# A decoder layer on one core: the norm's gain moved back into the weights, five leading chunks, and the sums of squares multiplied out later

## The chip, the core and the metric

The kernel runs on one NeuronCore of a Trainium2 chip. The core has a matrix engine (TensorE, called PE in the profile, with its weight loads as PEld), a vector engine (DVE), a scalar engine (ACT), a general engine (POOL) and a queue engine (SP) that issues DMAs. Each runs its own queue of instructions in order and waits for the others on semaphores. Results of PE go to eight PSUM banks; everything else lies in SBUF. The metric is the device time of one execution in microseconds; lower is better.

## The reference

One layer of a hybrid decoder, for a prompt of 1024 tokens and 8 sequences of 4 sample tokens (1056 token columns together), model width 1024, all in float32:

```python
h = x * rsqrt(mean(x*x) + EPS) * norm_g
b_g, c_g, u, z_a, v, z_b = split(h @ w_in)        # 1024 -> 6 x 512
y_a = b_g * conv3(c_g * u) * silu(z_a)            # three taps along the tokens
pooled = window_mean(v) - v                       # windows 2, 4, 8, 16 for four groups of 128
y_b = (pooled @ pool_w[group]) * pool_scale * silu(z_b)
out = rmsnorm(x + concat(y_a, y_b) @ w_out) * final_g
```

The last rows of `c_g*u` and of `v` are returned as new states. The row factor `rsqrt(...)` belongs to a token, `norm_g` to an input channel. So `norm_g` can be multiplied into x or into the rows of `w_in`, and the row factor can be applied after the projection.

## The kernel before, in words

**Numbers in two halves.** Every float32 operand of a product is split into a high half, which ACT writes with a copy in the rounded format fp32r, and a low half, which DVE writes as operand minus high half (`split2`, L155 to L158). A product takes three passes: high by low, low by high, high by high.

**The input projection.** Its 24 tiles of 128 output channels are taken in 12 pairs (`PAIRS`, L35). Tokens are cut in three ranges of 352 columns, n0, n1 and n2. Pair zero (v and z_b of group 0) is done straight, chunk by chunk of 128 input channels as they arrive: `project_first` (L190), chunks in four DMA groups of 1, 2, 2 and 3 (`GROUPS`, L109). Each chunk of x is multiplied with its gain while it is split (`split_x`, L169 to L173). Ranges n2 and n0 go along with the DMAs; n1 follows.

**Pairs one to eleven** use Strassen's scheme (Winograd's form) on n0 and n1 and plain products on n2. The weights of a pair (`wraw`, 1 MB, one buffer) give four split units: a and b from the weights, c and d from their differences `tw` (`make_t`, L207 to L216: one instruction of 1024 columns, two of 512). The x side needs A11, A12, A22 and the combinations S1 to S4, made once. On PE a block is 12 products of 352 columns. Pair p runs, in `strassen` (L418):

- block B11 with A11 into bank a; ACT copies it to s1 (L440)
- block T2 with S2 into bank b; DVE writes t1 = b + s1 (L444)
- block T1 with S1 into bank c
- a plain product of 24 into bank l (L450 multiplies it with the row factors)
- block B21 with A12 into a; L452 multiplies it with the row factors
- block T3 with S3 into b, which overwrites what t1 was read from; DVE writes t2 = b + s1 (L455)
- the second plain product into bank r; then T4 with A22 into b, B22 with S4 into c

In between, the hooks `early`, `middle` and `late` (L615 on) load the weights of pair p+1 and prepare its units.

**The row factors.** Rows of x are squared and summed on ACT for five tiles of 128 tokens (`square_rows`, L248). For the rest, ACT squares x in its other layout (`squares_head`, `squares_last`), DVE adds up (`sums_last`, `sums_head`), and PE sums over the partitions (`sums_rest`, L280 to L287). `rows` (L289) makes from this the factors and nine diagonal tiles; `rows_out` (L311) spreads them over the partitions with a product and copies them to R, and R squared to R2. This happens in pair two: sums right behind T1, row products behind the first plain product. Then `scale_heads` (L593) scales what pairs zero and one had left unscaled, and `after_u(0)` and `after_v(0)` do the convolution and the pooling of it.

**What sets the order.** Up to the end of pair one, PE, ACT, DVE and POOL follow the order of the text (`manual_schedule`, L489). From pair two on only PE does (L641); the instructions of ACT and DVE are put in order by the scheduler of the framework when the program is built, which mostly lets earlier text go first and fills holes with what is ready. The blocks of a pair are written behind one another; between the two parts the scheduler had already mixed some products of pair two's first block among the last of pair one.

Of the kernel before, what the change touches and what calls it, by code (L numbers as in the profile page):

```python
# [7 lines left out]
F32 = mybir.dt.float32  # L8
F32R = mybir.dt.float32r
AF = mybir.ActivationFunctionType  # L10
# [3 lines left out]
P = 128  # L14
# [18 lines left out]


PAIRS = [(("v", 0), ("zb", 0)), (("c", 0), ("u", 0)), (("za", 0), ("b", 0)),  # L35
# [3 lines left out]
NP = len(PAIRS)  # L39
M_ORDER = [t for pair in PAIRS for t in pair]  # L40
NF = 2
M_BASE = {"b": 0, "c": 512, "u": 1024, "za": 1536, "v": 2048, "zb": 2560}

E_ORDER = [0, 4, 7, 1, 6, 2, 5, 3]

WF = NF * P + 1

# [15 lines left out]
def trunk(ctx, tc, xt, xres, xct, w_first, w_in, w_out, pool_w, par, fg, sconv, spool,  # L63
# [17 lines left out]
    def tmp(name, dtype=F32):  # L81
        return tp.tile([P, TOK], dtype, tag="tmp", name=name)

    def snap(name):
        return sp.tile([P, TN], F32, tag="snap", name=name)

    def bank(name):
        return ps.tile([P, 512], F32, tag="ps", name=name)
# [17 lines left out]
        nc.sync.dma_start(raw[n][:, k:k + m, :], xt[:, n * KD + k:n * KD + k + m, :])  # L106


    GROUPS = ((0, 1), (1, 2), (3, 2), (5, 3))  # L109
    for k, m in GROUPS:  # L110
        nc.sync.dma_start(wfraw[:, k:k + m, :], w_first[:, k:k + m, :])
        for n in (2, 0):
            load_x(n, k, m)
# [41 lines left out]
    def split2(hi, lo, src):  # L155

        nc.scalar.activation(hi, src, AF.Copy)  # L157
        nc.vector.tensor_tensor(lo, src, hi.bitcast(F32), op=ALU.subtract)  # L158
# [7 lines left out]
    pl = [xtile("xh", "pl_0"), xtile("xi", "pl_1")]  # L166
    blocks = {(0, 0): A11, (0, 1): A12, (1, 0): A21, (1, 1): A22, (2, 0): pl[0], (2, 1): pl[1]}

    def split_x(n, k, g):  # L169
        dst, src = blocks[n, k // KH], raw[n][:, k]  # L170
        hi, lo = (dst[:, a, k % KH] for a in range(2))
        nc.scalar.activation(hi, src, AF.Copy, scale=g)
        nc.vector.scalar_tensor_tensor(lo, src, g, hi.bitcast(F32), op0=MUL, op1=SUB)  # L173


    def wtile(i, shape, name, dtype=F32R):
# [1 line left out]

    w0 = [wtile(h, [P, 2, KH, 2 * P], f"w0_{h}") for h in range(2)]

    def prep_w0(k0, m):
        for h in range(2):
            a, b = max(k0, h * KH), min(k0 + m, (h + 1) * KH)
            if a < b:
                q = slice(a - h * KH, b - h * KH)
                split2(w0[h][:, 0, q], w0[h][:, 1, q], wfraw[:, a:b, :2 * P])

    pm = {}

# [11 lines left out]


    unit = {}
    slot = {}
    tw = {}

    def make_t(p, steps=(0, 1)):  # L207
        w = wraw[p]
        if 0 in steps:
            tw[p] = wp.tile([P, 4, KH * P], F32, tag="tw", name=f"tw_{p}")  # L210
        t = tw[p]
        if 0 in steps:
            vt(t[:, 0:2], w[:, 2:4], w[:, 0::2], op=SUB)
        if 1 in steps:
            vt(t[:, 2], w[:, 3], t[:, 0], op=SUB)
            vt(t[:, 3], w[:, 1], t[:, 2], op=SUB)  # L216

    def make_unit(p, u):
        if p not in slot:
# [195 lines left out]

    def strassen(p, S1, S2, S3, S4, hooks):  # L418
        (q, j), (_, _) = PAIRS[p]
        if q == "v":  # L420
# [7 lines left out]
            left, right = tmp(f"z_{j}"), tmp(f"y_{j}")  # L428
            scale = R

        def plain(i, name):
            pt = bank(name)[:, :TN]
            block(pt, p, ("B11", "B12")[i], pl[0], True, False)
            block(pt, p, ("B21", "B22")[i], pl[1], False, True)
            return pt

        a = bank(f"a_{p}")[:, :TN]
        s1 = snap(f"s1_{p}")
        block(a, p, "B11", A11, True, False)
        nc.scalar.copy(s1, a)  # L440
        b = bank(f"b_{p}")[:, :TN]
        block(b, p, "T2", S2, True, False)
        t1 = snap(f"t1_{p}")
        vt(t1, b, s1, op=ADD)  # L444
        c = bank(f"c_{p}")[:, :TN]
        block(c, p, "T1", S1, True, False)
        hooks.get("rest", lambda: None)()
        pL = plain(0, f"l_{p}")
        hooks.get("rows", lambda: None)()
        vt(left[:, n2], pL, scale[:, n2], op=MUL)  # L450
        block(a, p, "B21", A12, False, True)
        vt(left[:, n0], a, scale[:, n0], op=MUL)  # L452
        block(b, p, "T3", S3, False, False)
        t2 = snap(f"t2_{p}")
        vt(t2, b, s1, op=ADD)  # L455
        vt(right[:, n1], c, t2, op=ADD)
        hooks["early"]()
        pR = plain(1, f"r_{p}")
        if q == "v":
            vt(right[:, n2], pR, R[:, n2], op=MUL)  # L460
        elif q == "c":
# [25 lines left out]
    szb[0] = tmp("szb_0")  # L487
    heads = [vb[:, PM:], szb[0]]
    with tc.manual_schedule(engines={ET.PE, ET.Activation, ET.DVE, ET.Pool}):  # L489
        for k0, m in GROUPS:  # L490
            prep_w0(k0, m)
            for k in range(k0, k0 + m):
                for n in (2, 0):
                    split_x(n, k, wfraw[:, k, 2 * P:])
                    project_first(n, k)
        nc.vector.tensor_copy(gain.rearrange("p (k o) -> p k o", o=1), wfraw[:, :, 2 * P:])
        gk = [gain[:, k:k + 1] for k in range(KD)]
        load_w(1)
        nc.sync.dma_start(part, par)
        xk = [load_rows(t, q[:, :D]) for t, q in enumerate((R, R2, up[:, 2:]))]  # L500
        slot[1] = {"a": 2, "b": 3, "d": 4, "c": 0}
        slot[2] = {"a": 1, "d": 2, "c": 0, "b": 4, "spare": 3}
        acc = tmp("acc")
        for k in range(KD):
            split_x(1, k, gk[k])
            project_first(1, k)
        sh = squares_head(acc)

        S3f, S2f, S1f = raw[1][:, :KH], raw[1][:, KH:], raw[0][:, :KH]
        vt(S3f, raw[0][:, :KH], raw[1][:, :KH], op=SUB)  # L510
        make_unit(1, "a")
        for k in range(KH):
            nc.scalar.activation(S3f[:, k], S3f[:, k], AF.Copy, scale=gk[k])
        for k in range(KH):
            nc.vector.scalar_tensor_tensor(S2f[:, k], S2f[:, k], gk[KH + k], S3f[:, k], op0=MUL, op1=SUB)
        make_t(1)
        make_unit(1, "b")
        for i in range(2):
            nc.scalar.copy(heads[i][:, n2], pm[i, 2])
        sq = squares_last()  # L520
        make_unit(1, "d")
        S2 = xtile("xa", "S2")
        split(S2, S2f)
        S3 = xtile("xb", "S3")
        split(S3, S3f)
        make_unit(1, "c")
        x34 = wtile(1, [P, 2, D], "x34", F32)
        xk += [load_rows(t, x34[:, t - 3]) for t in (3, 4)]
        load_w(2)
        for k in range(KH):  # L530
            nc.vector.scalar_tensor_tensor(S1f[:, k], S1f[:, k], gk[k], S2f[:, k], op0=MUL, op1=ADD)
        for t in (3, 4, 2):
            square_rows(t, xk[t])


        t_0, um = tmp("t_0"), up[:, 2:]

        def plain1(i):
            pt = bank(f"lr{i}_1")[:, :TN]
            block(pt, 1, ("B11", "B12")[i], pl[0], True, False)  # L540
            block(pt, 1, ("B21", "B22")[i], pl[1], False, True)
            return pt

        pL = plain1(0)
        pa, pb, pc = (bank(f"{q}_1")[:, :TN] for q in "abc")
        s1, t1, t2 = (snap(f"{q}_1") for q in ("s1", "t1", "t2"))
        block(pa, 1, "B11", A11, True, False)
        nc.scalar.copy(s1, pa)
        pR = plain1(1)
        block(pa, 1, "B21", A12, False, True)  # L550
        S4f = [tp.tile([P, 2, TN], F32, tag="tmp", name=f"S4f_{h}") for h in range(2)]
        for k in range(KH):
            nc.vector.scalar_tensor_tensor(S4f[k // 2][:, k % 2], raw[0][:, KH + k], gk[KH + k], S2f[:, k],
                                           op0=MUL, op1=SUB)
        S1 = xtile("xc", "S1")
        split(S1, S1f)
        make_unit(2, "a")
        for n in (0, 1):
            for i in range(2):
                nc.scalar.copy(heads[i][:, cols[n]], pm[i, n])  # L560
        block(pb, 1, "T2", S2, True, False)
        vt(t1, pb, s1, op=ADD)
        S4 = xtile("xd", "S4")
        for h in range(2):
            ks = slice(2 * h, 2 * h + 2)
            split2(S4[:, 0, ks], S4[:, 1, ks], S4f[h])
        block(pc, 1, "T1", S1, True, False)
        nc.scalar.copy(t_0[:, n2], pL)
        make_t(2, (0,))
        nc.scalar.copy(t_0[:, n0], pa)  # L570
        block(pb, 1, "T3", S3, False, False)
        vt(t2, pb, s1, op=ADD)
        vt(um[:, n1], pc, t2, op=ADD)
        make_t(2, (1,))
        make_unit(2, "d")
        for t in range(2):
            square_rows(t, xk[t])
        block(pb, 1, "T4", A22, False, True)
        vt(t_0[:, n1], pb, s1, op=ADD)
        make_unit(2, "c")  # L580
        block(pc, 1, "B22", S4, False, True)
        vt(um[:, n0], pc, t1, op=ADD)
        for _ in sums_last(acc, sq):
            pass
        sums_head(acc, sh)
        make_unit(2, "b")
        vt(up[:, 2 + 2 * TN:], pR, t_0[:, n2], op=MUL)
        vt(up[:, 2:2 + 2 * TN], um[:, both], t_0[:, both], op=MUL)
# [23 lines left out]
    def pair(p):  # L612
        nxt = p + 1 < NP

        def early():  # L615
            if nxt:
                load_w(p + 1)
                make_t(p + 1)
                make_unit(p + 1, "a")

# [235 lines left out]
```

## Time and profile before

| | us |
|---|---|
| runs | 380.45, 380.75, 379.07 (median 380.45) |
| the profiled execution | 380.98 |
| its span, first to last instruction | 379.2 |
| PE busy, share of the span | 367.1, 97% |
| DVE busy | 278.8, 74% |
| ACT busy | 147.0, 39% |
| mean granted clock of PE | 0.982 |

How to read it: all rows come from one execution. A row of instructions gives its start and length in us, the engine, the line, the operation, what it writes and reads, and in brackets how long the engine had been idle before it and what ended that. A row of a group (`... x11 | 13.4, 1221 |`) gives the count, the sum in us and the mean in ns. A row of a stretch (`60.00:62.00 ...`) gives its length, then the busy time of PE, PEld, DVE, ACT and POOL with their counts, the granted clock, the share of the DMA engines and GB/s. The chain rows give start, length and what the end of the execution hung on. A DMA row ends with the KB and the us from issue to landing. Instructions that follow on one engine overlap by some 0.09 us, so that four of 574 ns take 2.0 us.

### The profile page before, as it was taken

Reading aid. Unit: us, or ns where it says so; the run is one execution under the profiler, and the core shown is the slowest. Engines: PE = TensorE matmul, PEld = TensorE weight load, DVE = VectorE, ACT = ScalarE, POOL = GpSimd, SP = SyncE. Lnnn points to the kernel's source line nnn. Section 1 sums busy time; section 2 is a strip of 40 time slices with the busy share of each in tenths; the row PEclk is TensorE's granted clock in tenths of the full one; section 3 lists DMA queues with packets and bytes.
Section 4 is the critical chain, followed back from the end, with each engine's and each line's share of the span. In section 5 each row is a group of like instructions: output and inputs, shape, how many; then the busy total and the mean of one; then the engine's idle time right before and its main releaser. Section 6 shows DMA issues by size and latency. Waiting matters only on the chain.

```text
span 379.2 us, 5200 instructions
## 1 busy us (share of the span) xinstructions
PE 367.1 (97%) x2114; PEld 353.4 (93%) x2114; DVE 278.8 (74%) x433; ACT 147.0 (39%) x231; POOL 1.4 (0%) x7
## 2 busy tenths in 40 slices
PE   6999997999999999999999999999999999999993
PEld 3999996999999999999999999999998889999883
DVE  3899869799999986769797666969269628222593
ACT  4899751863323323133332322332069215111212
POOL 0000000000000000000000000000000000000000
PEclk9899997899999999999999999999999999999998
DMA  7975002111131310303040130404639923100042
GB/s 226 394 258 190 34 0 67 73 33 80 57 112 58 112 57 19 150 2 111 0 169 0 54 137 11 165 3 129 270 110 349 417 89 124 45 0 2 0 180 111
DMA packets 13079, 41.67 MB, mean 110 GB/s; under 512 B 3712, under 2 KB 4224, under 8 KB 11648
## 3 DMA queue, kind: packets, MB, share of 16 engines
q1 hardware_dynamic: 12912, 41.02, 29.2%
q8 instruction: 16, 0.26, 0.3%
q10 hardware_dynamic: 144, 0.33, 0.2%
q14 instruction: 7, 0.06, 0.0%
HBM read 32.92 MB, written 8.42 MB: 109 GB/s over the span
## 4 chain that ended last, share of the span: by engine, by line
PE 93%; DVE 3%; DMA 2%; ACT 1%; SPq 0%; issue 0%; DVEq 0%
PE b L238 16%; PE po L686 15%; PE l L238 11%; PE a L238 11%; PE c L238 10%; PE r L238 10%; PE pc L756 10%; PE pm L196 6%; PE lr L238 2%; PE pp L392 2%; DMA raw<-in_xt_dram 2%; ACT R L249 1%; PE rest L285 0%; DVE wc L158 0%; DVE sq L274 0%; ACT wd L157 0%
## 5 line engine op out<-in xcount | busy, mean ns | idle before, releaser
L686 PE MATMUL po<-wo,mix 128*128 128x512 f32 (+1 forms) x264 | 56.5, 374 | 0.0
L686 PEld LDWEIGHTS po<-wo,mix 128*128 128x128 f32 x264 | 46.3, 188 | 9.7 <-DVE mix L158 0.2
L238 PE MATMUL a<-A,wa 128*128 128x352 f32 x264 | 46.4, 324 | 0.0
L238 PEld LDWEIGHTS a<-A,wa 128*128 128x128 f32 x264 | 43.3, 188 | 0.0
L238 PE MATMUL l<-pl,wa 128*128 128x352 f32 x240 | 42.5, 335 | 0.0
L238 PEld LDWEIGHTS l<-pl,wa 128*128 128x128 f32 x240 | 41.0, 197 | 0.0
L238 PE MATMUL r<-pl,wb 128*128 128x352 f32 x240 | 40.4, 324 | 0.0
L238 PEld LDWEIGHTS r<-pl,wb 128*128 128x128 f32 x240 | 39.1, 188 | 0.0
L756 PE MATMUL pc<-mix,wo 128*128 128x416 f32 x192 | 36.5, 351 | 0.0
L756 PEld LDWEIGHTS pc<-mix,wo 128*128 128x128 f32 x192 | 35.9, 188 | 0.5
L238 PE MATMUL c<-S,wc 128*128 128x352 f32 x132 | 23.4, 324 | 0.0
L238 PE MATMUL c<-S,wb 128*128 128x352 f32 x132 | 23.1, 324 | 0.0
L238 PE MATMUL b<-S,wc 128*128 128x352 f32 x132 | 23.1, 324 | 0.0
L238 PE MATMUL b<-S,wd 128*128 128x352 f32 x132 | 23.1, 324 | 0.0
L238 PE MATMUL b<-A,wd 128*128 128x352 f32 x132 | 23.1, 324 | 0.0
L157 ACT ACTIVATE wd<-tw 128x1024 fp32r<-128x1024 f32 x11 | 11.7, 1062 | 28.4 <-PE a L238 20.7
L238 PEld LDWEIGHTS c<-S,wc 128*128 128x128 f32 x132 | 21.6, 188 | 0.3 <-DVE wc L158 0.3
L238 PEld LDWEIGHTS b<-S,wc 128*128 128x128 f32 x132 | 21.7, 188 | 0.0
L238 PEld LDWEIGHTS c<-S,wb 128*128 128x128 f32 x132 | 21.7, 188 | 0.0
L238 PEld LDWEIGHTS b<-S,wd 128*128 128x128 f32 x132 | 21.7, 188 | 0.0
L238 PEld LDWEIGHTS b<-A,wd 128*128 128x128 f32 x132 | 21.7, 188 | 0.0
L758 DVE TENSOR_TENSOR zc<-pc,zc 128x416 f32<-128x416 f32 x8 | 4.7, 591 | 18.6 <-PE pc L756 18.6
(198 smaller groups left out, 530.7 us busy)
## 6 DMA issues: line engine op xcount, KB each, us to landing
wraw<-in_w_in_dram SPq DMA_DIRECT2D x11, 1024.0 KB, 4.7
woraw<-in_w_out_dram SPq DMA_DIRECT2D x8, 512.0 KB, 5.6
zt<-in_xres_dram SPq DMA_DIRECT2D x5, 512.0 KB, 6.2
spill_b<-yb SPq DMA_DIRECT2D x4, 528.0 KB, 2.8
mixraw<-spill_b SPq DMA_DIRECT2D x4, 528.0 KB, 6.4
out_yt_dram<-zt SPq DMA_DIRECT2D x4, 512.0 KB, 2.6
zc<-in_xct_dram SPq DMA_DIRECT2D x4, 416.0 KB, 7.2
out_yc_dram<-zc SPq DMA_DIRECT2D x4, 416.0 KB, 2.4
```

Of the source, the lines that this page charges most:

```text
L157: nc.scalar.activation(hi, src, AF.Copy)
L196: nc.tensor.matmul(pm[i, n], w0[k // KH][:, a, k % KH, i * P:(i + 1) * P], blocks[n, k // KH][:, b, k % KH], start=k == 0 and s == 0, stop ...
L238: nc.tensor.matmul(pt, t[:, a, i, k * P:(k + 1) * P], x[:, b, k], start=first and s == 0, stop=last and s == len(seq) - 1, skip_group_chec ...
L249: nc.scalar.activation(xk, xk, AF.Square, accum_out=ss[:, t:t + 1])
L392: nc.tensor.matmul(pt[:, :TN], pws[:, a, g, :], pooled[g][b][:, cols[n]], start=(s == 0), stop=(s == 2))
L686: nc.tensor.matmul(pt, mix[k][:, b, t * P:(t + 1) * P], wo[k][:, a, c], start=(k == 0 and s == 0), stop=(k == KD - 1 and s == 2))
L756: nc.tensor.matmul(pt, wo[k][:, a, d * P:(d + 1) * P], mix[k][:, b, T0:], start=(k == 0 and s == 0), stop=(k == KD - 1 and s == 2))
L758: nc.vector.tensor_tensor(zc[d], pt, zc[d], op=ALU.add)
```

## The change

- **Gain.** x is split as it is. The first weights are multiplied with the gain while they are split (`prep_w0(k)`, chunk by chunk); for pairs one to eleven a new `gain_w(p)` multiplies the loaded weights in place, eight ACT instructions of 2 x 128 columns, ahead of `make_t` and of unit a. The scaled combinations of x become plain sums and differences, in larger pieces.
- **Chunks.** The leading DMA groups are 1, 1, 1, 2, 3.
- **Pair one.** S1 and the four parts of S4 are made earlier; the x rows of tiles 3 and 4 are loaded behind the squaring of tiles 0 and 1 into the same buffers; the second weights are loaded earlier; copies and squarings stand in another order. s1, t1 and t2 of pair one use the result tiles, so that pair two's first block (`first_a`) can be written ahead of pair one's T4.
- **Pair two.** The sums' products stand behind the first plain product instead of ahead of it; the row products stand in the middle of the second plain product; the two multiplications with R that stood ahead of it come behind it.
- **Groups of v.** Pairs three, six and nine take groups 1, 3, 2 instead of 3, 2, 1. Group g has g + 1 window sums.

```diff
-         (("v", 3), ("zb", 3)), (("c", 1), ("u", 1)), (("za", 1), ("b", 1)),
-         (("v", 2), ("zb", 2)), (("c", 2), ("u", 2)), (("za", 2), ("b", 2)),
-         (("v", 1), ("zb", 1)), (("c", 3), ("u", 3)), (("za", 3), ("b", 3))]
+         (("v", 1), ("zb", 1)), (("c", 1), ("u", 1)), (("za", 1), ("b", 1)),
+         (("v", 3), ("zb", 3)), (("c", 2), ("u", 2)), (("za", 2), ("b", 2)),
+         (("v", 2), ("zb", 2)), (("c", 3), ("u", 3)), (("za", 3), ("b", 3))]
...
-    GROUPS = ((0, 1), (1, 2), (3, 2), (5, 3))
-    for k, m in GROUPS:
+    for k, m in ((0, 1), (1, 1), (2, 1), (3, 2), (5, 3)):
...
+    def gain_w(p):
+        for k in range(KD):
+            t = wraw[p][:, 0::2] if k < KH else wraw[p][:, 1::2]
+            t = t[:, :, k % KH * P:(k % KH + 1) * P]
+            nc.scalar.activation(t, t, AF.Copy, scale=gain[:, k:k + 1])
...
-        hooks.get("rest", lambda: None)()
-        pL = plain(0, f"l_{p}")
-        hooks.get("rows", lambda: None)()
-        vt(left[:, n2], pL, scale[:, n2], op=MUL)
+        pL = plain(0, f"l_{p}")
+        hooks.get("rest", lambda: None)()
+        late = "rows" in hooks
+        if not late:
+            vt(left[:, n2], pL, scale[:, n2], op=MUL)
         block(a, p, "B21", A12, False, True)
-        vt(left[:, n0], a, scale[:, n0], op=MUL)
+        if not late:
+            vt(left[:, n0], a, scale[:, n0], op=MUL)
...
-        pR = plain(1, f"r_{p}")
+        pR = plain(1, f"r_{p}", hooks.get("rows"))
+        if late:
+            vt(left[:, n2], pL, scale[:, n2], op=MUL)
+            vt(left[:, n0], a, scale[:, n0], op=MUL)
...
-        for k0, m in GROUPS:
-            prep_w0(k0, m)
-            for k in range(k0, k0 + m):
-                for n in (2, 0):
-                    split_x(n, k, wfraw[:, k, 2 * P:])
-                    project_first(n, k)
+        for k in range(KD):
+            prep_w0(k)
+            for n in (2, 0):
+                split_x(n, k, 1)
+                project_first(n, k)
...
+        vt(S2f, raw[1][:, KH:], S3f, op=SUB)
+        vt(S1f, raw[0][:, :KH], S2f, op=ADD)
+        gain_w(1)
+        make_t(1)
         make_unit(1, "a")
...
+        S1 = xtile("xc", "S1")
+        split(S1, S1f)
+        gain_w(2)
         pR = plain1(1)
...
+        first_a(2)
         block(pb, 1, "T4", A22, False, True)
...
                 load_w(p + 1)
+                gain_w(p + 1)
                 make_t(p + 1)
                 make_unit(p + 1, "a")
```

More of the change, by code (lines that the diff above doesn't have):

```diff
@@ L42 @@
 M_BASE = {"b": 0, "c": 512, "u": 1024, "za": 1536, "v": 2048, "zb": 2560}
-E_ORDER = [0, 4, 7, 1, 6, 2, 5, 3]
+E_ORDER = [0, 4, 5, 1, 7, 2, 6, 3]
 WF = NF * P + 1
@@ L167, in trunk, with split_x @@
     blocks = {(0, 0): A11, (0, 1): A12, (1, 0): A21, (1, 1): A22, (2, 0): pl[0], (2, 1): pl[1]}
[L169 to L173, printed above, removed]
+    def split_x(n, k, m):
+        dst = blocks[n, k // KH]
+        ks = slice(k % KH, k % KH + m)
+        split2(dst[:, 0, ks], dst[:, 1, ks], raw[n][:, k:k + m])
     def wtile(i, shape, name, dtype=F32R):
@@ L179, in trunk, with prep_w0 @@
     w0 = [wtile(h, [P, 2, KH, 2 * P], f"w0_{h}") for h in range(2)]
[L181 to L186, printed above, removed]
+    def prep_w0(k):
+        t, q = w0[k // KH], k % KH
+        src, g = wfraw[:, k, :2 * P], wfraw[:, k, 2 * P:]
+        nc.scalar.activation(t[:, 0, q], src, AF.Copy, scale=g)
+        nc.vector.scalar_tensor_tensor(t[:, 1, q], src, g, t[:, 0, q].bitcast(F32),
+                                       op0=ALU.mult, op1=ALU.subtract)
     pm = {}
@@ L203, in trunk @@
     unit = {}
-    slot = {}
     tw = {}
+    def gain_w(p):
[3 more added lines that the diff above has]
+            nc.scalar.activation(t, t, AF.Copy, scale=gain[:, k:k + 1])
     def make_t(p, steps=(0, 1)):
@@ L216, in make_t @@
             vt(t[:, 3], w[:, 1], t[:, 2], op=SUB)
+    slot = {}
     def make_unit(p, u):
@@ L414, in after_u, with first_a @@
         keep["yc"] = yc
+    begun = {}
+    def first_a(p):
+        a = bank(f"a_{p}")[:, :TN]
+        s1 = snap(f"s1_{p}")
+        block(a, p, "B11", A11, True, False)
+        nc.scalar.copy(s1, a)
+        begun[p] = a, s1
     def strassen(p, S1, S2, S3, S4, hooks):
@@ L429, in strassen, with plain @@
             scale = R
-        def plain(i, name):
+        def plain(i, name, hook=None):
             pt = bank(name)[:, :TN]
             block(pt, p, ("B11", "B12")[i], pl[0], True, False)
+            if hook:
+                hook()
             block(pt, p, ("B21", "B22")[i], pl[1], False, True)
             return pt
[L437 to L440, printed above, removed]
+        if p not in begun:
+            first_a(p)
+        a, s1 = begun[p]
         b = bank(f"b_{p}")[:, :TN]
@@ L489, in trunk @@
     with tc.manual_schedule(engines={ET.PE, ET.Activation, ET.DVE, ET.Pool}):
-        for k0, m in GROUPS:
-            prep_w0(k0, m)
-            for k in range(k0, k0 + m):
-                for n in (2, 0):
-                    split_x(n, k, wfraw[:, k, 2 * P:])
-                    project_first(n, k)
+        for k in range(KD):
[3 more added lines that the diff above has]
+                project_first(n, k)
         nc.vector.tensor_copy(gain.rearrange("p (k o) -> p k o", o=1), wfraw[:, :, 2 * P:])
-        gk = [gain[:, k:k + 1] for k in range(KD)]
         load_w(1)
@@ L503, in trunk @@
         acc = tmp("acc")
+        for k in range(0, KD, 2):
+            split_x(1, k, 2)
         for k in range(KD):
-            split_x(1, k, gk[k])
             project_first(1, k)
@@ L510, in trunk @@
         vt(S3f, raw[0][:, :KH], raw[1][:, :KH], op=SUB)
+        vt(S2f, raw[1][:, KH:], S3f, op=SUB)
+        vt(S1f, raw[0][:, :KH], S2f, op=ADD)
+        gain_w(1)
+        make_t(1)
         make_unit(1, "a")
[L512 to L516, printed above, removed]
         make_unit(1, "b")
-        for i in range(2):
-            nc.scalar.copy(heads[i][:, n2], pm[i, 2])
+        load_w(2)
+        for n in (2, 0):
+            for i in range(2):
+                nc.scalar.copy(heads[i][:, cols[n]], pm[i, n])
         sq = squares_last()
         make_unit(1, "d")
+        S4f = [tp.tile([P, 2, TN], F32, tag="tmp", name=f"S4f_{h}") for h in range(2)]
+        for h in range(2):
+            ks = slice(2 * h, 2 * h + 2)
+            vt(S4f[h], raw[0][:, KH:][:, ks], S2f[:, ks], op=SUB)
         S2 = xtile("xa", "S2")
@@ L526, in trunk @@
         make_unit(1, "c")
[L527 to L533, printed above, removed]
         t_0, um = tmp("t_0"), up[:, 2:]
@@ L545, in trunk @@
         pa, pb, pc = (bank(f"{q}_1")[:, :TN] for q in "abc")
-        s1, t1, t2 = (snap(f"{q}_1") for q in ("s1", "t1", "t2"))
+        s1, t1, t2 = t_0[:, n1], um[:, n0], um[:, n1]
         block(pa, 1, "B11", A11, True, False)
         nc.scalar.copy(s1, pa)
+        square_rows(2, xk[2])
+        S1 = xtile("xc", "S1")
+        split(S1, S1f)
+        gain_w(2)
         pR = plain1(1)
         block(pa, 1, "B21", A12, False, True)
[L551 to L560, printed above, removed]
+        make_t(2, (0,))
         block(pb, 1, "T2", S2, True, False)
         vt(t1, pb, s1, op=ADD)
+        make_t(2, (1,))
         S4 = xtile("xd", "S4")
@@ L566, in trunk @@
             split2(S4[:, 0, ks], S4[:, 1, ks], S4f[h])
+        make_unit(2, "a")
+        for i in range(2):
+            nc.scalar.copy(heads[i][:, n1], pm[i, 1])
         block(pc, 1, "T1", S1, True, False)
         nc.scalar.copy(t_0[:, n2], pL)
-        make_t(2, (0,))
         nc.scalar.copy(t_0[:, n0], pa)
+        for t in range(2):
+            square_rows(t, xk[t])
+        xk += [load_rows(t, xk[t - 3]) for t in (3, 4)]
         block(pb, 1, "T3", S3, False, False)
         vt(t2, pb, s1, op=ADD)
+        make_unit(2, "d")
         vt(um[:, n1], pc, t2, op=ADD)
[L574 to L577, printed above, removed]
+        first_a(2)
         block(pb, 1, "T4", A22, False, True)
@@ L582, in trunk @@
         vt(um[:, n0], pc, t1, op=ADD)
+        for t in (3, 4):
+            square_rows(t, xk[t])
         for _ in sums_last(acc, sq):
```

## The prediction

> **What bounds the kernel now.** I read the page's head first, then the busy time by stretches, then the chain of waits in order of time.
>
> ```profile
> span 379.2 us, 5200 instructions
> PE 367.1 (97%) x2114; PEld 353.4 (93%) x2114; DVE 278.8 (74%) x433; ACT 147.0 (39%) x231; POOL 1.4 (0%) x7
> ```
> ```profile
> 6.50:9.00 2.50, 0.00 (x1) 0.00 (x0) 0.70 (x2) 1.22 (x2) 0.00 (x0) 1.00 0.98 354
> 11.00:12.00 1.00, 1.00 (x6) 1.00 (x5) 1.00 (x3) 1.00 (x4) 0.00 (x0) 0.50 1.05 427
> 60.00:62.00 2.00, 0.00 (x0) 0.00 (x0) 1.90 (x5) 0.00 (x0) 0.00 (x0) 0.87 0.00 0
> 62.30:68.30 6.00, 5.99 (x23) 5.96 (x24) 5.20 (x19) 2.57 (x11) 0.00 (x0) 0.50 0.59 217
> 82.60:280.40 197.80, 197.80 (x1226) 197.80 (x1225) 155.64 (x222) 61.66 (x80) 0.00 (x0) 1.00 0.23 83
> ```
> ```profile
> 32.09 3.88 PE lr L238 x24
> 35.97 1.94 PE a L238 x12
> ...
> 62.03 0.23 DVE acc L262
> ...
> 62.31 1.64 PE rest L285 x8
> 63.95 6.05 PE l L238 x24
> 70.00 0.97 PE pr L315 x6
> ...
> 82.61 1.94 PE a L238 x12
> ```
>
> PE is 97% busy. A block of 12 products takes 1.94 us and a plain product of 24 takes 3.88 us. From 82.6 us on PE never waits until the tail, so the change moves the end only by what it moves up to there, or by waits that it newly makes behind it. Ahead of 82.6 us PE loses time in two places. At 6.5 us it waits 2.5 us for the second chunk, and the clock is at 0.50 a little later. At about 59.5 us it waits 2.8 us for the sums of squares, and the granted clock is then 0.50 for 6 us: the first plain product of pair two takes 6.05 us in place of 3.88.
>
> **The change part by part.** *Leading chunks and gain in the first weights.* The rows:
>
> ```profile
> raw<-in_xt_dram SPq DMA_DIRECT2D x1, 176.0 KB, 2.5
> raw<-in_xt_dram SPq DMA_DIRECT2D x1, 352.0 KB, 5.8
> ```
> ```profile
> 15.44 0.59 ACT L172 ACTIVATE A<-raw,wfraw 128x352 fp32r<-128x352 f32 x1 [0.71 <-DMA raw<-in_xt_dram]
> 18.55 0.16 DVE L496 COPY gain<-wfraw 128x8 f32<-128x8 f32 x1
> 24.07 1.06 ACT L157 ACTIVATE wa<-wraw 128x1024 fp32r<-128x1024 f32 x1 [0.85 <-DMA wraw<-in_w_in_dram]
> ```
> ```profile
> L513 ACT ACTIVATE raw<-raw,gain 128x352 f32<-128x352 f32 x4 | 2.0, 574 | 0.0
> L157 ACT ACTIVATE w<-wfraw 128x256 fp32r<-128x256 f32 x3 | 1.1, 407 | 1.0 <-DMA wfraw<-in_w_first_dram 1.0
> L268 ACT ACTIVATE sq<-raw 128x1056 f32<-128x1056 f32 x2 | 2.1, 1084 | 0.0
> L519 ACT COPY szb<-pm 128x352 f32<-128x352 f32 x1 | 0.4, 447 | 0.0
> L213 DVE TENSOR_TENSOR tw<-wraw 128x1024 f32<-128x1024 f32 x11 | 13.4, 1221 | 2.5 <-DMA wraw<-in_w_in_dram 2.5
> L215 DVE TENSOR_TENSOR tw<-wraw,tw 128x512 f32<-128x512 f32 x11 | 7.6, 687 | 0.1
> L158 DVE TENSOR_TENSOR wa<-wraw,wa 128x1024 fp32r<-128x1024 f32 x11 | 13.4, 1221 | 0.2 <-ACT wa L157 0.2
> L158 DVE TENSOR_TENSOR S<-raw,S 128x1408 fp32r<-128x1408 f32 x3 | 4.8, 1623 | 1.6 <-ACT S L157 1.5
> ```
>
> Chunk one alone lands between 2.5 us after its issue (the single chunk) and 5.8 us (the double one); three more DMAs pass SP. I take the middle, about 7.0 us: PE starts again near 7.7 instead of 9.0, seven chunks of 1.94 us follow, and the last 48 products (7.8 us) end at 29.0. Bounds: 28.5 to 31.9, the latter no gain at all. But the next gate does not come sooner. The last x chunk still lands at 15.4, since the bytes are the same; behind it ACT now also prepares the weights of chunks six and seven, and its last half is done at 15.4 + 0.5 + 2 x 1.3 = 18.6, the gain copy on DVE at 19.35 (18.71 before). The first weights of pair one wait for that copy, because they use the same buffer, and take 5.3 us from issue (issued right behind the copy, they let ACT start at 24.07), so they land at 24.7.
>
> Now eight ACT products with the gain come first. No row shows one of 256 columns; the scaled one of 352 takes 574 ns, four in 2.0 us, the unscaled one of 256 takes 407 ns. Eight cost 2.7 us by the one and 3.9 us by the other; I take 3.1, nearer to the one of the same width. Then 24.7 + 3.1 = 27.8; the differences of the weights (1.22 + 2 x 0.69) end at 30.5 and the low half of the first unit (1.22) at 31.7. Pair one thus starts at 31.7 against 32.09: the start's gain is taken by a new wait of up to 2.7 us at this place.
>
> *Pair one.* In this order DVE goes on from 31.7: a low half (1.1), a wait for ACT to 34.9 (four copies of 0.4 and three squarings of 1 us now stand ahead of the next high half there), a low half, 1.6 for S4, two of 1.6 for S2 and S3, a low half, and at 42.1 the low half of S1, which needs ACT's high half behind S3: 43.8. ACT's second eight gain products lie at 42.0 to 45.2, then on DVE 1.2 + 0.5 + 1.4 (weight differences and t1), 1.7 (S4), 1.2 (unit a of pair two): 50.9. PE has by then waited 1.8 us for the moved first block of pair two. From 50.9 it runs five blocks (9.7) and the plain product that now lies ahead of the sums: 64.5. The sums on DVE, which took from 57.7 to 62.25 before (rows below and above, t1 of pair two among them), start near 57.4 now and end near 61.0. So that wait of 2.8 us and its slow clock go; the sums' products then take about 1.0 us at full clock, half of 1.64 and a little. They end at 65.5; before it was 63.95. Unknown: 1.5 us either way from the start's landing times, which go through the DVE queue unshortened.
>
> *The row scales.* What they still need, and what follows, stands in these rows:
>
> ```profile
> 57.74 1.25 DVE L274 TENSOR_TENSOR sq<-sq,sq 128x1056 f32<-128x1056 f32 x1
> ...
> 66.36 2.66 ACT L307 ACTIVATE diag<-ident,rh 128x128 fp32r<-128x128 f32 x9
> 69.59 1.23 DVE L213 TENSOR_TENSOR tw<-wraw 128x1024 f32<-128x1024 f32 x1 [1.20 <-DMA wraw<-in_w_in_dram]
> 70.36 1.17 ACT L316 COPY R<-pr 128x352 f32<-128x352 f32 x3 [1.34 <-PE pr L315]
> 84.38 2.10 PE L238 MATMUL b<-S,wd 128*128 128x352 f32 x12
> 92.37 0.52 DVE L444 TENSOR_TENSOR t<-b,s 128x352 f32<-128x352 f32 x1
> 94.09 2.10 PE L238 MATMUL b<-S,wc 128*128 128x352 f32 x12
> ```
> ```profile
> 69.60:92.40 22.80, 22.80 (x143) 22.80 (x142) 22.20 (x31) 13.69 (x21) 0.00 (x0) 1.00 0.13 47
> 82.60:94.10 11.50, 11.50 (x74) 11.50 (x73) 11.50 (x19) 5.96 (x9) 0.00 (x0) 1.00 0.26 93
> ```
>
> From the sums' products to the last diagonal it is 66.36 + 2.66 - 63.95 = 5.1 us, so 70.6 now; PE meanwhile has three blocks (5.8 us) and comes at 71.4: no wait. Three more blocks and the 0.97 of the row products put the end of pair two at 78.2, against 82.61: 4.4 us ahead.
>
> *Where it is given back.* DVE is the engine to look at behind this point. Between 69.6 and 92.4 it is busy 22.2 of 22.8 us, and what it does last there is the sum t1 of pair three (L444), which PE's block T3 of that pair overwrites and so waits for. It ends at 92.9; T3 starts at 94.1. PE can gain **1.2 us and no more** unless DVE starts this list sooner or orders it otherwise. It starts later. The list opens with the weight differences of pair three, and these now wait for eight gain products on ACT, which stand behind nine diagonals: 70.7 + 3.1 = 73.9 instead of 69.6. The copies of R come after the row products at 72.3, on the same ACT queue: 73.8 to 76, instead of 70.4 to 71.5, and most of the list needs R. Two sums of pair two (2 x 0.45) are done ahead of it. So t1 starts at 73.9 + 22.2 - 0.9 = 95.2, or 94.7 where holes close, and T3 starts at 95.3 to 95.8 where it was 94.1: **1.4 us later than before**. PE is there six blocks later than 78.2 (94.25 - 82.61 = 11.6), at 89.8, and waits more than 5 us.
>
> What the clock makes of that wait: idle stretches of 2.5 and 2.8 us were each followed by a clock near 0.5, once for about 3.4 us (a loss of 1.7) and once for 6.8. Here 0 to 2.8 us can be lost; I take 1.4. The Trainium skill (TensorE: Matmul & The Clock Gate, Part 1) has the clock halved after at least one idle window of about 3.4 us, in free-running windows. This trace is harsher: 2.8 us idle was enough. By that rule a wait of 5 us costs one window at half rate, 1.7 us where the sum has 1.4.
>
> *Gain products in the later pairs.* Eight per pair, 3.1 us of ACT. The cover:
>
> ```profile
> 154.80 1.06 ACT L157 ACTIVATE wa<-wraw 128x1024 fp32r<-128x1024 f32 x1 [2.84 <-DMA wraw<-in_w_in_dram]
> 157.76 0.69 DVE L216 TENSOR_TENSOR tw<-wraw,tw 128x512 f32<-128x512 f32 x1
> 161.26 1.06 ACT L157 ACTIVATE wd<-tw 128x1024 fp32r<-128x1024 f32 x1 [1.11 <-PE a L238]
> 172.64 2.10 PE L238 MATMUL b<-S,wd 128*128 128x352 f32 x12
> ```
>
> Weights that land at 154.8 would have their differences at 160.6 instead of 158.4; the unit made of them waits for PE until 161.26 in any case, and PE wants it at 172.6. Nothing is paid; without this cover it would be 3.1 us in each of nine pairs.
>
> *Order of the groups.* The group with four windows leaves the crowded pair three, the one with two takes its place: two window sums less of 1.23 us and their small ones, some 3 us of DVE, but behind t1 of pair three. It helps pair four, where PE had no wait: nothing.
>
> **Sum.** Against the profiled execution (380.98 us, 0.53 above the median of 380.45; span 379.2): +1.4 for T3 of pair three, +1.4 for the clock, nothing behind it: 383.8, or 383.2 on the scale of the median. Own range 381 to 386.
>
> **Rivals.** *Faster: the backlog does not bind.* Behind pair one only PE's order is written by hand; DVE's is chosen by the scheduler. If it places t1 and t2 of pair three ahead of the heads' scaling, done before PE comes at 89.8, the 4.4 us stay: 376.1, or 378 with half of them kept. For it: PE's part in this list is earlier. Against: t1 had been ready since T2 ended at 86.5, and ran at 92.37: older work went first.
>
> *No change: the list starts on time.* If the head runs 1.5 us faster than my sum and PE's wait stays under 2 us, the full slack of 1.2 is kept or lost again to a short slow clock: 379.3 to 381.5, say 380.3.
>
> *Slower still: gain products ahead of the diagonals.* The third weights land as far behind pair two's last unit as before (some 6 us), near 68.2, when the diagonals start (65.5 + 2.4). If they go first on ACT, the row products wait 3 us, R comes at 76, and T3 at 96.8: 380.45 + 2.7 + 2 = 385.
>
> **How the numbers follow.** Forecast 0.50, faster 0.25, no change 0.17, slower still 0.08. A measurement of this kernel tells 0.5%, 1.9 us, from no change. Slower: 0.40 of the forecast's 0.50 and the 0.08: 0.48. Faster: 0.25 and 0.02 of the no-change case: 0.27. The same: the rest, 0.25. The range for 8 in 10 leaves out the fullest gain and ends at the forecast's upper end: 377.5 to 386.
>
> **What would show it.** The first plain product of pair one starts near 31.7 behind `wa`, not near 29. No wait of PE at the sums (L285 of before). Pair two ends near 78. Then a wait of PE of 4 to 6 us on a DVE `t` in pair three, and a granted clock of 0.5 behind it. If PE runs through pair three without a wait, my backlog is wrong and the kernel is faster; if it waits in every pair on `tw` or `wd`, the cover of the gain products is.

## The result and the profile after

The kernel after takes 384.81 us (median of 384.53, 384.67, 384.96 and 385.07) against 380.60 us for the kernel before on the same chip (379.07 to 380.91): 1.0119 times as long, 95% interval 1.009 to 1.0147. It is slower by 1.2%, inside the predicted range, 1.6 us above the predicted 383.2. The profiled execution took 384.53 us.

The head of the page after: span, then busy time of each engine.

```profile
span 382.7 us, 5278 instructions
PE 365.7 (96%) x2114; PEld 351.0 (92%) x2114; DVE 276.5 (72%) x424; ACT 178.7 (47%) x314; POOL 1.4 (0%) x7
```

PE does as many instructions as before (x2114). ACT has 32 us more work, DVE 2 us less; no engine became full over the whole span. So the 3.5 us of span must be waits and clock. PE's list after, in order of time (start, length, what ran, in brackets the idle time before it):

```profile
29.43 0.43 PE L243 MATMUL lr<-pl,wa 128*128 128x352 f32 x1
32.18 3.99 PE L243 MATMUL lr<-pl,wa 128*128 128x352 f32 x23 [2.32 <-DVE wa L157]
51.66 2.04 PE L243 MATMUL a<-A,wa 128*128 128x352 f32 x11 [1.71 <-DVE wa L157]
...
65.18 0.88 PE L290 MATMUL rest<-one,acc 128*128 128x1 f32 x8
71.92 1.13 PE L320 MATMUL pr<-diag,onesr 128*128 128x352 f32 x6
78.71 2.10 PE L243 MATMUL a<-A,wa 128*128 128x352 f32 x12
88.50 2.10 PE L243 MATMUL a<-A,wa 128*128 128x352 f32 x12
95.58 3.89 PE L243 MATMUL b<-S,wc 128*128 128x352 f32 x12 [4.97 <-DVE t L459]
99.26 4.11 PE L243 MATMUL r<-pl,wb 128*128 128x352 f32 x24
```

The same two places in the list of before, the sums and the first block of pair three:

```profile
62.31 1.64 PE L285 MATMUL rest<-one,acc 128*128 128x1 f32 x8 [2.83 <-DVE acc L262]
...
82.45 2.10 PE L238 MATMUL a<-A,wa 128*128 128x352 f32 x12
```

The wait at the sums is gone (no bracket at L290), and pair three begins at 78.71 instead of 82.45, so PE is 3.7 us ahead. Then it stands still for 4.97 us in the middle of pair three, on the DVE sum t1 (L459), and block T3 comes at 95.58 where it came at 94.09. After that wait T3 takes 3.89 us, where a block of 12 takes 2.10 in this list. The stretches round it (length, then busy time of PE, PEld, DVE, ACT, POOL, then the granted clock):

```profile
29.80:32.20 2.40, 0.08 (x2) 0.02 (x1) 2.37 (x4) 2.40 (x6) 0.00 (x0) 1.00 0.00 0
62.30:68.30 6.00, 6.00 (x41) 5.97 (x40) 3.85 (x12) 0.78 (x5) 0.00 (x0) 1.00 0.49 178
66.00:74.00 8.00, 8.00 (x51) 8.00 (x50) 4.10 (x18) 6.48 (x22) 0.00 (x0) 1.00 0.20 84
90.60:95.58 4.98, 0.01 (x2) 0.01 (x1) 4.98 (x10) 3.88 (x8) 0.00 (x0) 0.70 0.00 0
95.58:99.47 3.89, 3.89 (x13) 3.89 (x14) 3.89 (x5) 0.95 (x3) 0.00 (x0) 0.51 0.34 139
```

The slow clock moved from 62.3 (0.50 before, 1.00 now) to 95.58 (0.51). While PE waits, DVE is busy 4.98 of 4.98 us: the late engine is DVE. But between 66 and 74 us the same DVE worked only 4.10 of 8.00 us. What it waited for there stands in the rows of DVE (first fence) and ACT (second):

```profile
70.73 0.52 DVE L473 TENSOR_TENSOR y<-c,t 128x352 f32<-128x352 f32 x1
74.04 1.23 DVE L216 TENSOR_TENSOR tw<-wraw 128x1024 f32<-128x1024 f32 x1 [2.79 <-ACT wraw L208]
...
94.99 0.53 DVE L459 TENSOR_TENSOR t<-b,s 128x352 f32<-128x352 f32 x1
```
```profile
24.98 3.31 ACT L208 ACTIVATE wraw<-wraw,gain 128x256 f32<-128x256 f32 x8 [3.18 <-DMA wraw<-in_w_in_dram]
...
68.15 2.67 ACT L312 ACTIVATE diag<-ident,rh 128x128 fp32r<-128x128 f32 x9
70.72 3.29 ACT L208 ACTIVATE wraw<-wraw,gain 128x256 f32<-128x256 f32 x8
73.92 0.43 ACT L321 COPY R<-pr 128x352 f32<-128x352 f32 x1
75.21 0.78 ACT L321 COPY R<-pr 128x352 f32<-128x352 f32 x2
```

DVE's list, from here on, is what it does from its first instruction that needs pair three's weights or R, up to t1. On ACT the gain products of pair three stand between the diagonals and the copies of R. Both things that can feed DVE's list, the gained weights and R, therefore come at 74 us or later. From 74.04 to the start of t1 it is 20.95 us, and DVE is busy in all of them.

### The profile page after: what moved, and what is told of

It reads as the page before. It is cut to its first block, busy times and chain, and to the rows that moved or that the text cites. A ratio compares the mean times of both kernels' runs of the same rounds, so it can differ in the third digit from the quotient of the medians.

```text
span 382.7 us, 5278 instructions
## 1 busy us (share of the span) xinstructions
PE 365.7 (96%) x2114; PEld 351.0 (92%) x2114; DVE 276.5 (72%) x424; ACT 178.7 (47%) x314; POOL 1.4 (0%) x7
## 4 chain that ended last, share of the span: by engine, by line
PE 73%; DVE 4%; issue 0%; ACT 0%; DVEq 0%
PE po L705 15%; PE b L243 14%; PE pc L775 10%; PE r L243 9%; PE c L243 9%; PE a L243 8%; PE l L243 8%; PE pp L397 2%; DVE yc L414 1%; DVE yc L418 0%; DVE up L613 0%; DVE vb L615 0%; DVE z L502 0%; DVE wb L157 0%; DVE pl L380 0%
## 5 line engine op out<-in xcount | busy, mean ns | idle before, releaser
L208 ACT ACTIVATE wraw<-wraw,gain 128x256 f32<-128x256 f32 x88 | 36.6, 496 | 17.4 <-DMA wraw<-in_w_in_dram 17.4
L243 PE MATMUL l<-pl,wa 128*128 128x352 f32 x240 | 40.4, 324 | 0.0
L243 PEld LDWEIGHTS l<-pl,wa 128*128 128x128 f32 x240 | 39.1, 188 | 0.0
L243 PE MATMUL b<-S,wc 128*128 128x352 f32 x132 | 25.0, 341 | 5.0 <-DVE t L459 5.0
L243 PEld LDWEIGHTS b<-S,wc 128*128 128x128 f32 x132 | 23.1, 201 | 5.3 <-DVE t L459 5.3
L216 DVE TENSOR_TENSOR tw<-wraw 128x1024 f32<-128x1024 f32 x11 | 13.5, 1226 | 16.7 <-ACT wraw L208 16.7
```

Of the source, the lines that this page charges most:

```text
L208: nc.scalar.activation(t, t, AF.Copy, scale=gain[:, k:k + 1])
L243: nc.tensor.matmul(pt, t[:, a, i, k * P:(k + 1) * P], x[:, b, k], start=first and s == 0, stop=last and s == len(seq) - 1, skip_group_chec ...
```

## The experiments

Each kernel was timed in five rounds beside the kernel before; the ratios are to that kernel's runs on the same chip, with 95% intervals. 0.1% is 0.38 us. The rows of PE, DVE and ACT quoted here read like those above.

**Without the gain in pair three.**

```diff
-                gain_w(p + 1)
+                if p != 2:
+                    gain_w(p + 1)
```

> The kernel after, without the eight gain products on pair three's weights (the gain is left out of that pair's columns, so its values are not the reference's). Theory: these 3.29 us, behind the diagonals on ScalarE, set where VectorE's list for pair three starts (74.04 us), and this list ends with the addition that lets pair three's T3 start (95.58). Then the list starts near 71, T3 starts at 92.0 to 92.7, the wait ahead of it shrinks from 4.97 to 1.5 to 2.2 us, and the time is 379.8 with T3 at full clock (381.8 if the clock still drops), so 379.3 to 382. Rival: the gain products cost something in every pair and pair three is one of eleven: 384.3 to 384.8, T3 still at 95 or later.

Measured: 380.76 us, ratio 1.0017 (0.9999 to 1.0034), against 1.0119 for the whole change. DVE's list first, then PE's:

```profile
69.72 1.22 DVE L216 TENSOR_TENSOR tw<-wraw 128x1024 f32<-128x1024 f32 x1
...
91.61 0.52 DVE L459 TENSOR_TENSOR t<-b,s 128x352 f32<-128x352 f32 x1
```
```profile
92.18 3.58 PE L243 MATMUL b<-S,wc 128*128 128x352 f32 x12 [2.04 <-DVE t L459]
```

The list starts at 69.72 with no idle time ahead of it (71 was expected), T3 at 92.18, as the theory had it, and in this execution T3 still ran at a slow clock (3.58 us in place of 2.10). Eight ACT instructions of 3.29 us together are worth 3.9 us (1.0%).

**Without the gain in the later pairs.**

```diff
-                gain_w(p + 1)
+                if p == 2:
+                    gain_w(p + 1)
```

> The kernel after, without the gain products of pairs four to eleven (the gain is left out of their columns); pairs one to three keep theirs. Theory: in these pairs 3.3 us of ScalarE lie beside 23 us of products on TensorE and cost nothing: 384.8, between 384.0 and 385.6, T3 of pair three at 95.6 as it was. Rival: each of the eight pairs pays some 0.5 us: 380.8 or less.

Measured: 384.81 us, ratio 1.0126 (1.0104 to 1.0147); T3 at 95.46 behind the same wait of 4.97 us. The other 64 gain products cost nothing that shows.

**Half of pair three's gain products on DVE.**

```diff
-            nc.scalar.activation(t, t, AF.Copy, scale=gain[:, k:k + 1])
+            if p == 3 and k % 2:
+                nc.vector.tensor_scalar(t, t, gain[:, k:k + 1], None, op0=MUL)
+            else:
+                nc.scalar.activation(t, t, AF.Copy, scale=gain[:, k:k + 1])
```

> The kernel after; of the eight gain products on pair three's weights VectorE, which has nothing to do there, takes four, and ScalarE keeps four. The same sums are computed. Theory: VectorE's list starts when its first feed is there, the gained weights or the row factors, whichever comes first; with half the products on each engine it starts near 72.4 in place of 74.04, T3 of pair three starts near 93.9 in place of 95.6, still behind a wait of over 3 us and at half clock: 383.2, between 381.8 and 384.2, that is between the whole kernel after (384.8) and the one without these products (380.8). Rival: it is not the start of the list that counts but the work in it, which grows by four products of some 0.4 us: 384.8 or more.

Measured: 382.82 us, ratio 1.008 (1.0063 to 1.0098). DVE's list, then PE's:

```profile
70.77 0.35 DVE L209 TENSOR_SCALAR wraw<-wraw,gain 128x256 f32<-128x256 f32 x1
72.17 1.22 DVE L219 TENSOR_TENSOR tw<-wraw 128x1024 f32<-128x1024 f32 x1 [0.36 <-ACT wraw L211]
...
93.14 0.51 DVE L462 TENSOR_TENSOR t<-b,s 128x352 f32<-128x352 f32 x1
```
```profile
31.48 5.52 PE L246 MATMUL lr<-pl,wa 128*128 128x352 f32 x23 [1.91 <-DVE wa L157]
93.71 3.62 PE L246 MATMUL b<-S,wc 128*128 128x352 f32 x12 [3.46 <-DVE t L462]
```

DVE does more work and the kernel is faster, because the work lies in a hole ahead of the list. From the start of the list to t1 it is 20.97 us, as in the kernel after.

**PE kept busy through the wait.**

```diff
+        if p == 3:
+            fill = bank("fill")
+            for _ in range(20):
+                nc.tensor.matmul(fill, wz[:, 0:P], wz, start=True, stop=True)
         block(b, p, "T3", S3, False, False)
```

> The kernel after, with twenty further bf16 products of 512 columns (about 4.3 us) on TensorE ahead of T3 of pair three, into a bank that nobody reads: TensorE is busy through most of the 4.97 us wait, and T3 waits for the same addition. Theory: T3 starts at the same 95.6 and takes 1.95 us in place of 3.89, since the half clock behind it comes from the idle ahead of it: 382.9, between 382.4 and 383.4. Rival: the half clock has another cause (a fixed window of the throttle): T3 still takes 3.9 us and the time stays at 384.8.

Measured: 382.68 us, ratio 1.0075 (1.0054 to 1.0095).

```profile
89.85 4.55 PE L473 MATMUL fill<-const-bfloat16-1.0 128*128 128x512 bf16 x20
94.98 2.20 PE L243 MATMUL b<-S,wc 128*128 128x352 f32 x12 [0.58 <-DVE t L459]
```

T3 still waits for t1, but takes 2.20 us: the half clock came from the idle time, and it is worth about 0.44%, 1.7 us. In this execution t1 itself came at 94.42, 0.57 us earlier than above, so a part of the difference may be that.

**PE taken off DVE's list.** In pair three alone ACT copies what the three additions read:

```diff
-        vt(t1, b, s1, op=ADD)
+        nc.scalar.copy(t1, b)
+        vt(t1, t1, s1, op=ADD)
...
-        vt(t2, b, s1, op=ADD)
-        vt(right[:, n1], c, t2, op=ADD)
+        nc.scalar.copy(t2, b)
+        nc.scalar.copy(right[:, n1], c)
+        vt(t2, t2, s1, op=ADD)
+        vt(right[:, n1], right[:, n1], t2, op=ADD)
```

> The kernel after; in pair three alone ScalarE copies the sums that VectorE's three additions read (b after T2, b after T3, c after T1) out of their banks, and VectorE adds from the copies, so that TensorE no longer waits for VectorE's list to reach these additions. Three copies of 0.45 us more on ScalarE, VectorE's work unchanged. Theory: T3 starts at 90.6 with no wait and full clock, pair three's T4 and B22 follow, and pair four waits for its first weights until 102 to 103.5; the lead that pair two won is kept but for that: 379, between 378 and 381. Rival: another thing holds pair three (its own weights, a bank) and the list only named the wait: 383 or more, with a wait of over 3 us ahead of T3 or of the next block.

Measured: 379.59 us, ratio 0.9999 (0.9985 to 1.0012).

```profile
89.67 2.10 PE L243 MATMUL b<-S,wc 128*128 128x352 f32 x12
91.61 4.04 PE L243 MATMUL r<-pl,wb 128*128 128x352 f32 x24
...
101.75 2.04 PE L243 MATMUL a<-A,wa 128*128 128x352 f32 x11 [0.62 <-DVE wa L157]
105.06 2.04 PE L243 MATMUL b<-S,wd 128*128 128x352 f32 x11 [1.11 <-DVE wd L157]
```

T3 starts at 89.67 with no wait. DVE does no less work; it is only no longer what PE waits for. All of the 1.2% is back, although PE now waits 1.7 us in pair four for its weights. The three copies were put in together, so what each is worth alone is not known.

The same copies in the kernel before:

> The kernel before with the three ScalarE copies in pair three alone, and nothing moved. Theory: before the change TensorE did not wait for VectorE's list in pair three, so there is nothing to take away: 380, between 379.2 and 380.8, and the 3 to 4 us between this kernel and the one with both the copies and the moved sums (376.1) are what the move is worth where VectorE's list does not take it back. Rival: the copies are worth the 3 us by themselves: 377.

Measured: 379.96 us, ratio 1.0006 (0.999 to 1.0023). Before the change the copies are worth nothing.

**The moved sums and rows alone, in the kernel before.** The edit is the part of the change in `strassen` shown in the diff above.

> The kernel before with one part of the change: the sums' products behind pair two's plain product, the row products in the middle of its second plain product, the two scalings behind both. Theory: the wait of 2.83 us at the sums and the half clock behind it go, pair two ends near 77 in place of 82.45, TensorE then waits over 5 us ahead of T3 of pair three, which starts at 94 to 95 as before, and T3 runs at half clock: the whole lead is lost and 2 us with it: 382.5, between 380.6 and 384. Rival: the lead is kept, and the loss in the whole change comes from the gain products alone: 376, at most 378.

Measured: 379.10 us, ratio 0.9974 (0.9956 to 0.9993): neither expectation. PE's list, then DVE's:

```profile
76.10 2.10 PE L238 MATMUL a<-A,wa 128*128 128x352 f32 x12
90.79 3.54 PE L238 MATMUL b<-S,wc 128*128 128x352 f32 x12 [2.89 <-DVE t L446]
```
```profile
68.09 1.22 DVE L213 TENSOR_TENSOR tw<-wraw 128x1024 f32<-128x1024 f32 x1
...
90.21 0.52 DVE L446 TENSOR_TENSOR t<-b,s 128x352 f32<-128x352 f32 x1
```

Pair two ends 6.35 us earlier (82.45 to 76.10), and I had T3 fixed at 94. But without gain products the list starts at 68.09, 1.5 us earlier than before, and t1 is there at 90.21: T3 comes 3.3 us earlier, and the half clock behind a wait of 2.89 us takes 1.4 of that back (the next block starts at 94.17, 3.38 us behind T3's start, in place of 1.94).

**The same with the copies.**

> The kernel before with the same part (sums' products, row products and scalings moved) and in pair three the three ScalarE copies that take TensorE off VectorE's list. Theory: pair three runs from 77 with no wait ahead of T3, pair four waits for its first weights until about 101 to 102.5, 3 to 5 us earlier than before: 377, between 375.5 and 379. Rival: the move is worth nothing by itself: 380 or more.

Measured: 376.09 us, ratio 0.9904 (0.9886 to 0.9923). T3 starts with no wait:

```profile
87.84 2.10 PE L238 MATMUL b<-S,wc 128*128 128x352 f32 x12
```

This version beats both kernels: by 1.0% the one before, and the one after takes 1.022 times as long (1.0119 / 0.9904). Against the copies alone (1.0006) the move is worth 1.0%, 3.9 us, where DVE's list doesn't take it back.

**The sums and rows put back, in the kernel after.**

> The kernel after with the sums' products, the row products and the two scalings put back where they were before. Theory: TensorE waits 2 to 3 us at the sums again with half clock behind it, pair two ends 4 to 6 us later (83 to 85), but pair three's T3 cannot start before 95 anyway and finds little or no wait there, so the move is worth next to nothing in the whole change: 384.8, between 383.3 and 386.5. Rival: the move is worth the 3.9 us by which pair two ended earlier, and the rest of the change costs 8: 388 or more.

Measured: 380.94 us, ratio 1.003 (1.0014 to 1.0046): 3.4 us faster than the whole change, a miss of both expectations. PE's list, then ACT's, then DVE's:

```profile
62.38 0.98 PE L290 MATMUL rest<-one,acc 128*128 128x1 f32 x8 [1.18 <-DVE acc L267]
63.29 5.67 PE L243 MATMUL l<-pl,wa 128*128 128x352 f32 x24
...
81.42 2.10 PE L243 MATMUL a<-A,wa 128*128 128x352 f32 x12
...
93.92 2.10 PE L243 MATMUL b<-S,wc 128*128 128x352 f32 x12
```
```profile
69.33 1.16 ACT L321 COPY R<-pr 128x352 f32<-128x352 f32 x3 [0.24 <-PE pr L320]
70.36 0.53 ACT L208 ACTIVATE wraw<-wraw,gain 128x256 f32<-128x256 f32 x1
```
```profile
70.52 0.53 DVE L463 TENSOR_TENSOR z<-l,R 128x352 f32<-128x352 f32 x1 [2.08 <-ACT R L321]
...
92.46 0.53 DVE L457 TENSOR_TENSOR t<-b,s 128x352 f32<-128x352 f32 x1
```

The gain products are all there. But the row products come earlier, the scheduler puts the copies of R ahead of the gain products, and DVE starts its list at 70.52 with the work that needs R instead of the weights. T3 is at 93.92 with no wait, and takes the normal 2.10 us.

So the loss belongs to neither part. Ratios to before: the move alone 0.9974; all the rest of the change (gain, chunks, pair one, v order) without the move 1.003; both together 1.0119. The gain was not run alone; the chunks alone, further down, cost as much in the kernel before as all that rest. The list's start and t1's, in us:

| kernel | first feed of the list | list starts | t1 starts | T3 starts |
|---|---|---|---|---|
| move alone | weights, no gain | 68.09 | 90.21 | 90.79 |
| after, no gain in pair three | weights, no gain | 69.72 | 91.61 | 92.18 |
| after, sums and rows put back | R | 70.52 | 92.46 | 93.92 |
| after, half the gain on DVE | weights | 72.17 | 93.14 | 93.71 |
| after | weights | 74.04 | 94.99 | 95.58 |

In each of them 21.0 to 22.1 us lie between the start of the list and t1.

**The two small parts, together and one by one, in the kernel before.**

> The kernel before with the two small parts of the change: leading chunks of 1, 1, 1, 2 and 3, and the v groups in the order 0, 1, 3, 2 with the order of the output to match. Theory: neither is on the path: 380.6, between 379.8 and 381.4, with T3 of pair three at 94.1. Rival: the chunks bring the first products forward or the v order shifts the later pairs: a difference of over 1 us to either side.

> The kernel before with the v groups in the order 0, 1, 3, 2 alone, the order of the output to match. Theory: the later pairs have room for either order: 380, within 0.6 us of the kernel before. Rival: it carries the 0.9 us by which the kernel with both small parts was slower: 380.5 to 381.

> The kernel before with the leading chunks of 1, 1, 1, 2 and 3 alone. Theory: the wait at the first projections gets shorter by 1.6 us and the time comes back as waits in pair one: 380, within 0.8 us of the kernel before. Rival: it carries the 0.9 us by which the kernel with both small parts was slower: 380.5 to 381.

Measured: both 380.54 us, ratio 1.0029 (1.0009 to 1.005); the v order 379.53 us, 0.9999 (0.9985 to 1.0014); the chunks 380.35 us, 1.0028 (1.0012 to 1.0045). The v order is nothing. The chunks cost about 1 us. In the profiled execution with the chunks PE's wait ahead of the second chunk (2.51 us before) shrinks to one of 0.64 at a later chunk, and waits of 0.23 and 1.70 us turn up in pair one instead, the longer one because S1 is late. That gains nothing, but doesn't explain a whole us; what does is open, and so is whether the chunks cost as much in the kernel after.

## Why the prediction held, step by step

- *Start and first weights.* PE restarted at 6.66, not 7.7, and waited 0.91 us for a later chunk; the first projections ended at 29.4 (predicted 29.0), weights landed at 25.0 (24.7). Eight gain products took 3.31 us (3.1 taken; 496 ns each, between the two bounds). Pair one: 32.18 against 31.7, the new wait 2.32 us against "up to 2.7". "The start's gain is taken by a new wait" holds. That finer chunks alone would cost 0.28% was not in it.
- *Pair one.* The wait at the moved first block: 1.71 us at 51.66, predicted 1.8 at 50.9.
- *Sums and rows.* No wait at the sums, products 0.88 us (1.0), row products at 71.92 with no wait (71.4), pair two's end at 78.71 (78.2). Ahead by 3.7 us where I had 4.4: 0.5 us because the head ran later, and the rest because I took 82.61 from the chain for a block that starts at 82.45 in the list. The difference had no effect, since T3 waited for DVE and not for PE.
- *Where it is given back.* Right in place, engine and size: list at 74.04 (73.9), t1 at 94.99 (94.7 to 95.2), T3 at 95.58 (95.3 to 95.8). What I had not seen is that the list needs only one of its two feeds in time. I named both as late, but both are late only because the row products moved back and the gain products stand ahead of R's copies; the experiments with one part each were needed to show it, and my expectations for two of them were wrong for that reason.
- *Clock.* The undersized term: 1.4 us, the middle of a range of 0 to 2.8, so that it came near is partly luck. From T3's start to that of the next block it was 3.68 us (99.26 - 95.58) in place of 1.94: 1.74 lost, and the run with PE kept busy won about 1.7 back.
- *Later pairs, v order.* Both nothing, as forecast (1.0126 without the later gain products; 0.9999).
- *The sum.* In the profiled executions 3.55 us (384.53 - 380.98) against 2.8: 0.34 from the clock, 0.1 from T3 (1.49 for 1.4), 0.3 open. The other 0.85 us of the 1.6 by which the median was missed are the place of the profiled runs: the forecast took off 0.53 us because that of before lay so far above its median, but that of after lay 0.28 below its own; the rest is rounding.
- *Rivals.* "The backlog does not bind" falls: DVE had no idle time up to t1 at 94.99. "The list starts on time" falls: it started at 74.04. "Gain products ahead of the diagonals" falls: they stood behind them (70.72).

## What to carry to other kernels

A wait that is removed ahead of an engine that is full from there on only moves to that engine, so look for the last thing that the full engine's list does, and what starts the list. Here the list had two feeds and bore one of them late; two edits that cost little or nothing alone each took one feed. The cure that was worth most was not less work on the full engine but taking the other engine off it: three copies of 0.44 us by ScalarE, which had room for them, released TensorE's banks and were worth 1.2%.

## What the runs showed of the hardware that I had not expected

A short idle stretch can halve the clock or not, at the same length. At the start of pair one, the kernel with sums and rows put back (first fence) and the one with the filled wait (second), whose code is the same up to there:

```profile
31.49 5.52 PE L243 MATMUL lr<-pl,wa 128*128 128x352 f32 x23 [1.86 <-DVE wa L157]
```
```profile
31.60 3.99 PE L243 MATMUL lr<-pl,wa 128*128 128x352 f32 x23 [1.91 <-DVE wa L157]
```

A wait of 1.86 us was followed by 5.52 us of products (granted clock 0.50 from 33 to 36 us), one of 1.91 us by 3.99 (1.00 there); with half the gain on DVE, 1.91 us gave 5.52, and after, 2.32 us gave 3.99. The Trainium skill (TensorE: Matmul & The Clock Gate, Part 1) describes free-running windows of about 3.4 us; that the place of the wait decides fits these rows. Its condition, a whole window of idle time, doesn't: waits of under 2 us were enough here.

The place of such windows may differ from run to run, and a kernel's spread may come from it; no run here shows that directly. On record are the twelve runs with the move alone, which went from 377.54 us at a mean granted clock of 0.996 to 380.06 at 0.988. That is 0.67% for one kernel, so a difference of under 0.5% between two profiled executions of these kernels says little by itself.

A gain product of 2 x 128 columns takes 496 ns on ACT and 0.35 us on DVE.
